# A two-layer decoder trunk in fp32: three of four MLP up blocks by seven quarter products per pair of units, and the MLP's weight sums on GpSimd

## The chip, the cores and the metric

One core of one Trainium2 chip. The metric is the device time of one execution, in microseconds (us). PE is TensorE, PEld its weight loads, DVE VectorE, ACT ScalarE, POOL GpSimd, SP SyncE, which here issues most DMAs.

## The reference

512 tokens, width 1024, two layers. Each layer ends in an MLP; the rest (a DeltaNet branch, a sliding-window attention branch, their merge) is not touched by the change.

```python
h2 = rmsnorm(x, pre_mlp_g)                                  # 512 x 1024
ff = jnp.square(jax.nn.relu(h2 @ w_ff1)) @ w_ff2            # 1024 -> 4096 -> 1024
return x + rmsnorm(ff, post_mlp_g)
```

## The kernel before

**Products.** All large products are fp32 work as three matmuls: an operand x is split into x_h (rounded by a cast) and x_l = x - x_h, and a product is wh·x_h + wh·x_l + wl·x_h. Weights come in chunks of 128 x 1024 (512 KB). Each goes the same way: a DMA by SP into a buffer `wr` (WR = 5 of them), a cast by ACT to `wh` (L323), a subtraction by DVE to `wl` (L324), then PE. `wh` and `wl` have LOOK = 4 buffers each, so a chunk's cast waits until PE has released the chunk four before it. `chunk_order` lists all chunks, `specs` is that list, and every `weights()` call takes the next prepared chunk and emits cast and subtraction of one further on.

**The MLP.** The 4096 middle columns are four stripes s = 0 to 3 of 1024. A stripe has an *up block*, the product with w_ff1: eight units of 128 middle columns, each 24 matmuls of 512 tokens (`mm_a`, L339 to L341), written to a PSUM bank of tag "pm" (two banks); ACT takes relu (L1374) and square (L1375) into a tile `raw`. In stripe 0 the first four units are made early, in two halves of 256 tokens (`mm_a2`, L350 to L352).

For s < 3 a *down stage* follows, the product with that stripe's 1024 rows of w_ff2. It is a Strassen-Winograd scheme over quarters of the activation and of the weights: seven products P1 to P7 instead of eight, each of two chunks, 168 matmuls in all (`mm_c`, L400 to L404). `lefts` makes the left operands from `raw` (S1 to S4 on DVE, each then split by an ACT cast L411 and a DVE subtraction L412). `seven` makes the right operands: sums of loaded chunks, eight DVE additions of 128 x 1024 per stage (L293). Results are accumulated into `acc` (L1332, L1389, L1393, L1401, L1403, L1409). Stripe 3 has a plain down product (`mm_b4` and `last_tiles`), whose operands `h3` are split in the up block.

**What sets the order.** Where no order is written out by hand (`Order`), the framework's scheduler orders each engine's instructions; an engine then runs its queue in that order and stops at an instruction whose inputs aren't there. A matmul into a PSUM bank waits until readers of that bank that are ahead of it in the program are done.

Of the kernel before, what the change touches and what calls it, by code (L numbers as in the profile page):

```python
# [41 lines left out]
WR = 5  # L42
FF_ORDER = (0, 4, 1, 5, 2, 6, 3, 7)
XB = 6

# [7 lines left out]
def chunk_order(depth):  # L53


    out = []
    for l in range(depth):
        a_in = lambda w, c: out.append(("chunk", w, l, 0, c, 0))
        b_in = lambda w, r, c, n: out.append(("chunk", w, l, r, c, n))
        for n in range(3):  # L60
            for j in range(4):
                b_in("w_in", j * 256, OFF_B + n * NB, NB)
        n_ = {"K": 0, "G": 0, "A": 0}
        for c in "".join(MIX):
# [12 lines left out]
        for m in range(KT):  # L77
            a_in("w_up_dn", m * P)
        for n in range(2):
            for j in range(4):  # L80
                b_in("w_o", j * 256, n * 512, 512)
        for s in range(4):
            for m in FF_ORDER if s < 3 else range(8):
                a_in("w_ff1", (s * 8 + m) * P)
            if s < 3:
                out.append(("seven", "w_ff2", l, s * 1024))
                continue
            for n in range(2):
                for j in range(4):
                    b_in("w_ff2", s * 1024 + j * 256, n * 512, 512)  # L90
    return out


def chunk_keys(depth):

    keys = {}
    for kind, *key in chunk_order(depth):
        if kind == "chunk":
            keys[tuple(key)] = None
        else:  # L100
# [19 lines left out]
def hybrid_trunk(ctx, tc, x, positions, pre_mix_g, dn_conv_w, dn_a_log, dn_dt_bias, dn_norm_g,  # L120
# [155 lines left out]

    def blocks(a, n_):
        return a[:, :2 * n_ if n_ else 1024].rearrange("p (k c) -> p k c", k=2 if n_ else 8)

    def seven(w, l, r0):  # L280
# [11 lines left out]
        def add(i, k, j):  # L292
            tt(out=held[j], in0=held[j], in1=part(i, k, j), op=ALU.add)  # L293
            return held[j]

        makes = (lambda j: take(0, 0, j),
                 lambda j: add(0, 1, j),
                 lambda j: add(1, 1, j),
                 lambda j: add(1, 0, j),
                 lambda j: (take(0, 1, j), add(1, 1, j))[1],  # L300
                 lambda j: part(1, 0, j),
                 lambda j: part(1, 1, j))
        return [(lambda f=f, j=j: f(j), 512) for f in makes for j in range(2)]


    specs = []
    for kind_, *key in chunk_order(depth):
        if kind_ == "seven":
            specs.extend(seven(*key))
        else:  # L310
            specs.append((tuple(key), key[4]))
# [3 lines left out]
    def prefetch(n, wr=None, sub=tt):  # L315
        while len(pre) < min(n, len(specs)):
# [5 lines left out]
            w = 2 * n_ if n_ else 1024  # L322
# [83 lines left out]

    def four(i):
        return [b("ps_b4") for b in ((PZ, PZ, PS, PS) if i % 2 else (PM, PM, PK, PS))]
# [34 lines left out]
    def norm_half(xt, gb, r, g):  # L443

        xs = T[7]("xs")
        stt(out=xs, in0=xt[:, g * 512:(g + 1) * 512], scalar=r, in1=gb[g], op0=ALU.mult, op1=ALU.mult)
        return xs
# [22 lines left out]
    def post_tiles(tiles, a0g, ps1, add1, q0, gb, xsrc, xdst, gb2=None):  # L470
# [4 lines left out]
        xt = [[T[5 + i]("xt") for i in range(2)] for t in tiles]  # L475
# [22 lines left out]
        if gb2 is not None:  # L498
            q = [(meansq(xo[i][:, :512], "nq0"), meansq(xo[i][:, 512:], "nq1")) for i in n]
            for i in n:  # L500
                r = rstd("nr", *q[i])
                xs.append([norm_half(xo[i], gb2, r, g) for g in range(2)])
# [17 lines left out]
    for l in range(depth):  # L520
# [817 lines left out]
        def ff2_tail(tiles, pss):  # L1338
            a0, a1 = [a[0] for a in acc], [a[1] for a in acc]
            if l == depth - 1:  # L1340
                post_tiles(tiles, a0, pss, a1, s0, gb3, xd, give)
            else:
                xs_next.extend(post_tiles(tiles, a0, pss, a1, s0, gb3, xd, keep, nxt[0]))

        def lefts(X, Y):

            a11, a21, a12, a22 = X[:, 0:512], X[:, 512:1024], Y[:, 0:512], Y[:, 512:1024]
            S = {n_: T[4](n_) for n_ in ("S1", "S2", "S3", "S4")}
            tt(out=S["S1"], in0=a21, in1=a22, op=ALU.subtract)
            tt(out=S["S2"], in0=a11, in1=S["S1"], op=ALU.subtract)  # L1350
            for name, U, src in (("P1", T[5], a11), ("P5", T[7], S["S1"]), ("P6", T[1], S["S2"]),
                                 ("P4", T[2], a22), ("P7", T[3], S["S3"]), ("P2", T[6], a12),
                                 ("P3", T[0], S["S4"])):
                if name == "P4":
                    tt(out=S["S4"], in0=a12, in1=S["S2"], op=ALU.subtract)
                    tt(out=S["S3"], in0=a21, in1=a11, op=ALU.subtract)
                p_ = pair(U, name)
# [3 lines left out]
        for s in range(3):  # L1361
            left = {f"P{i}": [] for i in range(1, 8)}
            raw = [None, None]
            for i, m in enumerate(FF_ORDER):
                if s == 0 and i < 4:
                    ps = early[i][0]
                else:
                    ps = PM("ps_f1")
                    mm_a(ps, h2)

                if i % 4 < 2:
                    raw[i % 2] = X4("raw")
                r_ = raw[i % 2].rearrange("p (a k n) -> p a k n", a=2, k=2)[:, :, m % 2, :]
                act(out=r_, in_=ps.rearrange("p (a n) -> p a n", a=2), func=AF.Relu)  # L1374
                act(out=r_, in_=r_, func=AF.Square)  # L1375
                if i % 4 == 3:
                    lefts(*raw)
            pa, pb_ = [PZ("ps_p1") for t in range(2)], [PS("ps_p5") for t in range(2)]
            mm_c(pa, left["P1"])
            v_ = [T[4]("p1") for t in range(2)]  # L1380
            for t in range(2):
                nc.scalar.copy(v_[t], pa[t])
            mm_c(pb_, left["P5"])
            for t in range(2):
                into(2 + t, 1, pb_[t])
            pc = [PS("ps_p6"), PK("ps_p6")]
# [7 lines left out]
            pc = [PM("ps_p4"), PM("ps_p4")]  # L1394
# [3 lines left out]
            pc = [PS("ps_p7"), PK("ps_p7")]  # L1398
# [5 lines left out]
            mm_c(pa, left["P2"], True)  # L1404
            for t in range(2):
                into(t, 0, pa[t])
            mm_c(pb_, left["P3"], True)
            for t in range(2):
                tt(out=acc[t][1], in0=pb_[t], in1=acc[t][1], op=ALU.add)  # L1409


        gb3 = gain(post_mlp_g[l])
        h3 = []
        for m in range(8):
            ps = PM("ps_f1")
            mm_a(ps, h2)
            r_ = T[4]("relu")
            act(out=r_, in_=ps, func=AF.Relu)
            act(out=r_, in_=r_, func=AF.Square)
            p_ = pair(T[m % 4], "h3")  # L1420
            split(r_, *p_)
            h3.append(p_)
# [43 lines left out]
```

## Time and profile before

| what | us |
|---|---|
| median of 3 runs (lowest to highest) | 1831.27 (1830.51 to 1831.94) |
| span of the profiled execution | 1828.6 |
| an up block of layer 0, stripes 1 to 3 | 43.5 each |
| a down stage of layer 0, stripes 1 and 2 | 38.6 each |
| PE busy in the span | 1809.1 |
| DVE, ACT, POOL busy | 1292.1, 940.9, 211.2 |

The profiled execution's own time is not listed apart from the three runs; its span lies 2.7 us under their median. A row of a timeline reads: start, length, engine, line, operation, output <- inputs, shape, and in brackets how long the engine had been idle and for what. A row of a group reads: busy us, mean ns of one, and the idle time ahead of them. PE's records overlap, since matmuls are pipelined: the step between starts is what one costs.

### The profile page before, as it was taken

To read this page: it belongs to the slowest core of one execution; us is meant where nothing else is said; L and a number is where in the kernel's file an instruction comes from. 1 tells how busy PE (TensorE), PEld (TensorE's weight loads), DVE (VectorE), ACT (ScalarE), POOL (GpSimd) and SP (SyncE) were. 2 spreads that over 40 slices of the span, in tenths; PEclk is the share of its full clock that TensorE was granted. 3 is DMA by queue.
4 is the path that set the end of the run, shared out by engine and by line. 5 is a ranking of instruction groups with operands and counts; after the bars stand their busy time and mean duration, and the time that the engine had idled before them with its cause. 6 is when DMAs were issued, how large, how long until landed. Compare 5 with 4: busy or idle time off the path is not lost.

```text
span 1828.6 us, 26748 instructions
## 1 busy us (share of the span) xinstructions
PE 1809.1 (99%) x9598; PEld 1503.9 (82%) x9598; DVE 1292.1 (71%) x2466; ACT 940.9 (51%) x1913; POOL 211.2 (12%) x386
## 2 busy tenths in 40 slices
PE   9999999999999999999999999999999999999998
PEld 8888778888788888888898887888887898888886
DVE  5499796887566758684556997968885568585934
ACT  6678742444434645544347877234444346554442
POOL 0322102221101000000003221022111010000000
PEclk9999999999999999999999999999999999999999
DMA  5633447554453363564245343485545534544631
GB/s 188 202 118 116 115 149 223 179 170 149 124 191 124 96 216 120 168 217 151 93 151 181 104 127 110 167 234 165 160 139 153 172 119 135 174 163 148 233 102 46
DMA packets 146422, 278.48 MB, mean 152 GB/s; under 512 B 33569, under 2 KB 66657, under 8 KB 146290
## 3 DMA queue, kind: packets, MB, share of 16 engines
q1 hardware_dynamic: 145778, 276.75, 47.4%
q8 instruction: 75, 1.23, 0.3%
q14 instruction: 57, 0.47, 0.1%
q0 software_dynamic: 512, 0.03, 0.0%
HBM read 239.38 MB, written 37.36 MB: 151 GB/s over the span
## 4 chain that ended last, share of the span: by engine, by line
PE 84%; DVE 6%; ACT 5%; DMA 3%; issue 1%; POOL 1%; SPq 0%; POOLq 0%; DVEq 0%; ACTq 0%
PE ps_f L340 6%; PE ps_f L339 6%; PE ps_f L341 6%; PE ps_p L402 3%; PE ps_p L404 3%; PE ps_p L400 3%; PE ps_b L388 3%; PE ps_b L387 3%; PE ps_b L389 3%; PE ps_vp L339 2%; PE ps_us L339 2%; PE ps_ud L339 2%; PE ps_vp L341 2%; PE ps_ud L341 2%; PE ps_ud L340 2%; PE ps_us L340 2%
## 5 line engine op out<-in xcount | busy, mean ns | idle before, releaser
L323 ACT CAST wh<-wr 128x1024 fp32r<-128x1024 f32 (+1 forms) x332 | 343.1, 1040 | 542.2 <-PE ps_f L340 145.8
L324 DVE TENSOR_TENSOR wl<-wr,wh 128x1024 fp32r<-128x1024 f32 (+1 forms) x332 | 400.4, 1216 | 303.6 <-ACT wh L323 300.6
L339 PE MATMUL ps_f<-g_h,wh 128*128 128x512 f32 x448 | 174.3, 389 | 0.0
L340 PE MATMUL ps_f<-g_l,wh 128*128 128x512 f32 x448 | 174.3, 389 | 0.0
L341 PE MATMUL ps_f<-g_h,wl 128*128 128x512 f32 x448 | 174.3, 389 | 0.0
L402 PE MATMUL ps_p<-wl,P_h 128*128 128x512 f32 x336 | 131.4, 391 | 0.4 <-DVE wl L324 0.3
L404 PE MATMUL ps_p<-wh,P_l 128*128 128x512 f32 x336 | 130.8, 389 | 0.0
L400 PE MATMUL ps_p<-wh,P_h 128*128 128x512 f32 x336 | 129.5, 389 | 0.0
L437 POOL TENSOR_TENSOR pr<-pq,pw 128x1 f32<-128x1 f32 x16 | 9.8, 613 | 807.6 <-DVE pq L436 807.6
L339 PEld LDWEIGHTS ps_f<-g_h,wh 128*128 128x128 f32 x448 | 84.1, 188 | 17.4
L341 PEld LDWEIGHTS ps_f<-g_h,wl 128*128 128x128 f32 x448 | 84.1, 188 | 17.4
L340 PEld LDWEIGHTS ps_f<-g_l,wh 128*128 128x128 f32 x448 | 84.1, 188 | 17.4
L402 PEld LDWEIGHTS ps_p<-wl,P_h 128*128 128x128 f32 x336 | 63.1, 188 | 15.8 <-DVE wl L324 2.4
L400 PEld LDWEIGHTS ps_p<-wh,P_h 128*128 128x128 f32 x336 | 63.1, 188 | 13.3
L404 PEld LDWEIGHTS ps_p<-wh,P_l 128*128 128x128 f32 x336 | 63.1, 188 | 12.8
L387 PE MATMUL ps_b<-wh,h_h 128*128 128x432 f32 (+1 forms) x192 | 71.1, 370 | 0.0
L388 PE MATMUL ps_b<-wl,h_h 128*128 128x432 f32 (+1 forms) x192 | 70.5, 367 | 0.3 <-DVE wl L324 0.3
L389 PE MATMUL ps_b<-wh,h_l 128*128 128x432 f32 (+1 forms) x192 | 70.2, 366 | 0.0
L293 DVE TENSOR_TENSOR wr<-wr 128x1024 f32<-128x1024 f32 x48 | 58.0, 1220 | 2.6 <-DMA wr<-in_weights_dram 1.9
L340 PE MATMUL ps_qp<-h_l,wh 128*128 128x512 f32 x128 | 54.0, 422 | 0.0
L339 PE MATMUL ps_vp<-h_h,wh 128*128 128x512 f32 x128 | 53.9, 421 | 0.0
L341 PE MATMUL ps_vp<-h_h,wl 128*128 128x512 f32 x128 | 53.6, 419 | 0.0
(359 smaller groups left out, 4873.6 us busy)
## 6 DMA issues: line engine op xcount, KB each, us to landing
wr<-in_weights_dram SPq DMA_DIRECT2D x320, 512.0 KB, 3.5
wr<-in_weights_dram SPq DMA_DIRECT2D x24, 432.0 KB, 3.6
D<-dd SPq DMA_DIRECT2D x32, 256.0 KB, 3.2
xd<-xo SPq DMA_DIRECT2D x12, 512.0 KB, 2.8
xt<-xd SPq DMA_DIRECT2D x24, 256.0 KB, 3.7
D<-gd SPq DMA_DIRECT2D x16, 256.0 KB, 6.5
dd<-D SPq DMA_DIRECT2D x16, 256.0 KB, 3.9
kkd<-kk SPq DMA_DIRECT2D x16, 256.0 KB, 2.0
```

The lines of the kernel that those rows point to most:

```text
L293: tt(out=held[j], in0=held[j], in1=part(i, k, j), op=ALU.add)
L323: nc.scalar.copy(wh[:, :w], wr[:, :w])
L324: sub(out=wl[:, :w], in0=wr[:, :w], in1=wh[:, :w].bitcast(F32), op=ALU.subtract)
L339: mm(ps, lhsT=wh[:, k, :], rhs=hi, start=k == 0, stop=False)
L340: mm(ps, lhsT=wh[:, k, :], rhs=lo, start=False, stop=False)
L341: mm(ps, lhsT=wl[:, k, :], rhs=hi, start=False, stop=k == KT - 1)
L387: mm(pss[t], lhsT=hi[:, tsl], rhs=wh[:, r, :], start=k == 0, stop=False)
L388: mm(pss[t], lhsT=hi[:, tsl], rhs=wl[:, r, :], start=False, stop=False)
L389: mm(pss[t], lhsT=lo[:, tsl], rhs=wh[:, r, :], start=False, stop=k == KT - 1)
L400: mm(pss[t], lhsT=hi[:, c], rhs=wh[:, r, :], start=first, stop=False, skip_group_check=onto)
L402: mm(pss[t], lhsT=hi[:, c], rhs=wl[:, r, :], start=False, stop=False, skip_group_check=onto)
L404: mm(pss[t], lhsT=lo[:, c], rhs=wh[:, r, :], start=False, stop=last, skip_group_check=onto)
```

## The change

Stripes 1 to 3 get `ff1_pairs` in place of eight `mm_a`. Two units (256 middle columns) and two halves of 256 tokens make a 2 x 2 scheme of quarters: the weights' quarters are halves of the 1024 inputs by unit, the tokens' operands are a11, a12, a22 (quarters of h2, split already) and four combinations n1 to n4. Each of the seven products (`mm_h`) has 12 matmuls of 256, so a pair has 84 of them, and a block 336 of 256 instead of 192 of 512.

The results that several quarters share are not added by DVE but continued in PSUM: ACT copies A's result a0 into one of two "seed" banks (y, L1461), D is added onto it there, ACT copies that into the other seed bank (z, L1470), and so on. Two more matmuls of 512 per layer start the seed banks. q0 (product F) stands in the second half of the bank that holds a0 (except in a block's first pair, where it has a bank of its own) and is copied to SBUF (L1467, L1476). The products B and C of a pair are made after A of the next one (`finish`).

Weights: of each pair two raw chunks are loaded, and GpSimd makes four sums of 128 x 512 from them (L336, `paired`); four chunks go to PE per pair: one raw, two of sums, and a half one ("tail"). The sums in `seven` go from DVE to GpSimd too (L304). WR is 7 instead of 5.

The combinations: `combos` makes them in stripe 0 by eight GpSimd additions of 128 x 1024 per layer, with splits on ACT and DVE; n4 takes the place of h2's fourth quarter.

In the down stage P2 moves from sixth to third place; of P2, P7 and P3 the splits for both halves are now emitted inside the down stage (`make_later`); other PSUM tags and other tile tags (T[...]) are used.

```diff
-WR = 5
+WR = 7
+PAIRS = (((0, 1), (4, 5), (2, 3), (6, 7)), ((0, 1), (2, 3), (4, 5), (6, 7)))
...
         def add(i, k, j):
-            tt(out=held[j], in0=held[j], in1=part(i, k, j), op=ALU.add)
+            ptt(out=held[j], in0=held[j], in1=part(i, k, j), op=ALU.add)
...
+    def paired(l, s):
...
+                    for o_, i0, i1 in ((ya, x0, x2), (yb, ya, x3), (yd, x2, x3), (yc, yb, x1)):
+                        ptt(out=o_, in0=i0, in1=i1, op=ALU.add)
...
+        for n, ms in enumerate(PAIRS[s == 3]):
+            raw, fa, fb, tail = one(*ms)
+            out.append((raw, 0))
+            if last:
+                out.append((last, -1))
+            out += [(fb, 0), (fa, 0)] if n == 0 else [(fa, 0), (fb, 0)]
+            last = tail
...
+    def mm_h(ps, w, k0, op, start):
+
+        wh, wl = w
+        for k in range(4):
+            hi, lo = op[k]
+            mm(ps, lhsT=wh[:, k0 + k, :], rhs=hi, start=start and k == 0, stop=False,
+               skip_group_check=True)
+            mm(ps, lhsT=wh[:, k0 + k, :], rhs=lo, start=False, stop=False, skip_group_check=True)
+            mm(ps, lhsT=wl[:, k0 + k, :], rhs=hi, start=False, stop=k == 3, skip_group_check=True)
...
+        def ff1_pairs(done):
...
+            for n, ms in enumerate(PAIRS[s == 3]):
+                R = X4("raw")
+                y, z = (b[:, half(n % 2)] for b in seeds)
+                ps = PM("ps_f1")
+                a0, q0 = ps[:, half(0)], ps[:, half(1)]
+                q_ = sm.tile([P, 256], F32, name="q7")
+                c1 = weights()
+                mm_h(a0, c1, 0, ops["a11"], True)
+                nc.scalar.copy(y, a0)
+                finish()
+                if n == 0:
+                    q0 = PM("ps_f1")[:, half(1)]
+                    c3 = weights()
+                    mm_h(q0, c3, 4, ops["n3"], True)
+                    nc.scalar.copy(q_, q0)
+                c2 = weights()
+                mm_h(y, c2, 4, ops["n2"], False)
+                nc.scalar.copy(z, y)
+                mm_h(a0, c1, 4, ops["a12"], False)
+                act(out=R[:, half(0)], in_=a0, func=AF.Relu)
+                if n > 0:
+                    c3 = weights()
+                    mm_h(q0, c3, 4, ops["n3"], True)
+                    nc.scalar.copy(q_, q0)
+                mm_h(z, c2, 0, ops["n1"], False)
+                stt(out=R[:, half(3)], in0=z, scalar=-1.0, in1=q_, op0=ALU.mult, op1=ALU.subtract)
+
+                def finish(n=n, ms=ms, R=R, y=y, z=z, q_=q_, c3=c3):
+                    mm_h(y, c3, 0, ops["a22"], False)
+                    tt(out=R[:, half(2)], in0=y, in1=q_, op=ALU.add)
+                    act(out=R[:, 512:], in_=R[:, 512:], func=AF.Relu)
+                    mm_h(z, weights(), 0, ops["n4"], False)
+                    act(out=R[:, half(1)], in_=z, func=AF.Relu, scale=-1.0)
+                    act(out=R, in_=R, func=AF.Square)
+                    done(n, ms, R)
+            finish()
```

What stands on the engines, at three places. First ACT's queue in the up block of stripe 1, layer 0. Before (line 323 is a weight cast, 1374 and 1375 relu and square of a unit, 411 the cast of a down operand):

```order
L323 CAST wh_7220<-wr_7218 128x1024
L1374 ACTIVATE raw_7147<-ps_f1_7184 128x2x256
L1375 ACTIVATE raw_7147<-raw_7147 128x2x256
L411 CAST P1_h_7256<-raw_7147 128x512
L323 CAST wh_7289<-wr_7287 128x1024
L1374 ACTIVATE raw_7181<-ps_f1_7217 128x2x256
L1375 ACTIVATE raw_7181<-raw_7181 128x2x256
```

In the changed kernel, from the second pair's copy of D into z to the third pair's copy of F (373 is a weight cast, 471 the cast of a down operand; ps_f1_7371 is the bank that holds the third pair's a0 and q0):

```order
L373 CAST wh_7373<-wr_7335 128x1024
L1483 ACTIVATE raw_7248<-raw_7248 128x512
L373 CAST wh_7408<-wr_7404 128x1024
L1485 ACTIVATE raw_7248<-seed_7154 128x256
L1486 ACTIVATE raw_7248<-raw_7248 128x1024
L1470 COPY seed_7154<-seed_7153 128x256
L471 CAST P4_h_7442<-raw_7248 128x512
L373 CAST wh_7448<-wr_7284 128x512
L471 CAST P5_h_7433<-S1_7430 128x512
L471 CAST P6_h_7438<-S2_7431 128x512
L1472 ACTIVATE raw_7370<-ps_f1_7371 128x256
L1476 COPY q7_7372<-ps_f1_7371 128x256
```

A unit's relu stood directly behind one cast. Now the relu of a0 (L1472) stands behind ten instructions that belong to the pair before and to later chunks.

Second, PE's queue at the place of that relu, in the fourth pair of the same block. First before, at the border of two units:

```order
L340 MATMUL ps_f1_7184<-g_l_5939,wh_7098 128x512
L341 MATMUL ps_f1_7184<-g_h_5938,wl_7099 128x512
L339 MATMUL ps_f1_7217<-g_h_5936,wh_7119 128x512
L340 MATMUL ps_f1_7217<-g_l_5937,wh_7119 128x512
L341 MATMUL ps_f1_7217<-g_h_5936,wl_7120 128x512
```

And in the changed kernel, at the border of E (operands g, bank ps_f1_7515) and F (operand n3, the same bank); two matmuls of the next down stage (line 450) stand between them:

```order
L464 MATMUL ps_f1_7515<-g_l_5939,wh_7408 128x256
L465 MATMUL ps_f1_7515<-g_h_5938,wl_7409 128x256
L450 MATMUL ps_p1_7687<-wh_7568,P1_h_7426 128x512
L450 MATMUL ps_p1_7688<-wh_7568,P1_h_7426 128x512
L462 MATMUL ps_f1_7515<-n3_h_6637,wh_7517 128x256
L464 MATMUL ps_f1_7515<-n3_l_6638,wh_7517 128x256
L465 MATMUL ps_f1_7515<-n3_h_6637,wl_7518 128x256
```

Two units followed each other in different banks. F follows E in the bank that L1472 reads in between.

Third, the weight sums in the down stage of stripe 1, layer 0. Before, on DVE (324 is a chunk's subtraction, 293 a sum of two chunks, 412 a down operand's low part):

```order
L412 TENSOR_TENSOR P7_l_7275<-S3_7252,P7_h_7274 128x512
L293 TENSOR_TENSOR wr_7321<-wr_7321,wr_7388 128x1024
L324 TENSOR_TENSOR wl_7358<-wr_7355,wh_7357 128x1024
L293 TENSOR_TENSOR wr_7355<-wr_7355,wr_7461 128x1024
L324 TENSOR_TENSOR wl_7392<-wr_7321,wh_7391 128x1024
L293 TENSOR_TENSOR wr_7321<-wr_7321,wr_7480 128x1024
```

In the changed kernel, on POOL:

```order
L304 TENSOR_TENSOR wr_7566<-wr_7566,wr_7644 128x1024
L304 TENSOR_TENSOR wr_7598<-wr_7598,wr_7691 128x1024
L304 TENSOR_TENSOR wr_7566<-wr_7566,wr_7757 128x1024
L304 TENSOR_TENSOR wr_7598<-wr_7598,wr_7786 128x1024
L304 TENSOR_TENSOR wr_7847<-wr_7847,wr_7849 128x1024
L304 TENSOR_TENSOR wr_7566<-wr_7566,wr_7805 128x1024
L304 TENSOR_TENSOR wr_7598<-wr_7598,wr_7828 128x1024
L304 TENSOR_TENSOR wr_7882<-wr_7882,wr_7884 128x1024
L336 TENSOR_TENSOR wr_7969<-wr_7943,wr_7945 128x512
L336 TENSOR_TENSOR wr_7970<-wr_7945 128x512
```

The same eight sums of a stage stand in a row on POOL, and the next block's pair sums (L336) behind them; DVE keeps the subtractions.

More of the change, by code (lines that the diff above doesn't have):

```diff
@@ L1409, in hybrid_trunk, with done @@
                 tt(out=acc[t][1], in0=pb_[t], in1=acc[t][1], op=ALU.add)
+            if s == 0:
+                next(cg, None)
+        s = 3
         gb3 = gain(post_mlp_g[l])
[L1413 to L1422, printed above, removed]
+        h3 = [None] * 8
+        def done(n, ms, R):
+            for i, m in enumerate(ms):
+                h3[m] = pair(T[(1, 2, 5, 7)[m % 4]], "h3")
+                split(R.rearrange("p (a k n) -> p a k n", a=2, k=2)[:, :, i, :],
+                      *(a.rearrange("p (a n) -> p a n", a=2) for a in h3[m]))
+        ff1_pairs(done)
         pss = four(1)
```

193 lines of the change are left out of this document (145 added, 48 removed).

## The prediction

> **What bounds the kernel now.** I read the page first, then the busy time of each engine stage by stage (the table of windows), then PE's waits. The page's heads and the first row of its chain:
>
> ```profile
> span 1828.6 us, 26748 instructions
> ...
> PE 1809.1 (99%) x9598; PEld 1503.9 (82%) x9598; DVE 1292.1 (71%) x2466; ACT 940.9 (51%) x1913; POOL 211.2 (12%) x386
> ...
> PEclk9999999999999999999999999999999999999999
> ...
> PE 84%; DVE 6%; ACT 5%; DMA 3%; issue 1%; POOL 1%; SPq 0%; POOLq 0%; DVEq 0%; ACTq 0%
> ```
>
> TensorE never stands still and never loses its clock. The table of windows, for layer 0: the up block of stripe 1, its down stage, and the up block of stripe 3.
>
> ```profile
> core 0: us, PE busy (x) PEld busy (x) DVE busy (x) ACT busy (x) POOL busy (x), PEclk, DMA share, GB/s
> 664.17:707.69 43.52, 43.52 (x194) 36.04 (x192) 21.66 (x25) 20.80 (x31) 0.00 (x0) 1.00 0.34 106
> 707.69:746.25 38.56, 38.37 (x169) 31.40 (x168) 37.28 (x45) 19.63 (x24) 0.00 (x0) 1.00 0.58 196
> ...
> 828.33:871.85 43.52, 43.52 (x194) 36.04 (x192) 15.95 (x18) 20.70 (x30) 0.00 (x0) 1.00 0.39 135
> ```
>
> An up block is bound by PE alone: 43.52 us for 192 matmuls of 512, 226.7 ns each, DVE and ACT half idle. In the down stage DVE is busy 97% (37.28 of 38.56 us): no room there. From 575 to 900 us, which holds the MLP of layer 0, PE's waits are all of these:
>
> ```profile
> PE ps_p L402 <- DVE wl L324: 0.3, 2, 0.2
> PE ps_n L457 <- DVE g_l L463: 0.2, 1, 0.2
> ```
>
> So whatever shortens PE's stream in an up block shortens the kernel, as long as nobody makes PE wait; and any wait added there is paid in full.
>
> **The saving.** Six up blocks go from 192 matmuls of 512 to 336 of 256. What a 256 wide one costs stands in the early units' stream on PE (the ends are modelled, so I read starts):
>
> ```profile
> 578.82 0.28 PE L350 MATMUL ps_f<-g_h,wh 128*128 128x256 f32 x1
> ...
> 585.89 0.28 PE L352 MATMUL ps_f<-g_h,wl 128*128 128x256 f32 x1
> ...
> 589.53 0.36 PE L350 MATMUL ps_f<-g_h,wh 128*128 128x256 f32 x1
> 589.73 0.28 PE L351 MATMUL ps_f<-g_l,wh 128*128 128x256 f32 x1
> ```
>
> From the first to the second row are 59 steps in 7.07 us: 119.8 ns, a little over half of 226.7. So 336 x 0.1198 = 40.25 us against 43.52: 3.27 us less in a block, 19.6 in six. A product (12 matmuls) lasts 1.44 us. The last two rows show the first step after a stop, 0.20 instead of 0.12 us.
>
> The Trainium skill ("TensorE: Matmul & The Clock Gate", Back-to-back issue gap) lists 262 cycles for a 256 wide matmul and 518 for 512. At its 2.4 GHz that would be an estimated 109.2 and 215.8 ns and a saving of 28 us. The trace disagrees with both figures (119.8 and 226.7), and the sum goes by the trace.
>
> The two seed matmuls per layer add 4 x 0.227 = 0.9 us.
>
> **The waits that come, in the up blocks.** The order lists seven products per pair of units. I call them by their right operand: A (a11), B (a22) and C (n4) of the pair before, D (n2), E (a12), F (n3), G (n1). In the later three pairs of a block two of them wait for ACT.
>
> B adds into the seed bank into which ACT has just copied A's result (L1461). F writes the second half of the PSUM bank whose first half ACT must first read, with the relu of E's result (L1472). In ACT's queue this relu stands behind everything that B, C, D and E release. ACT's steps have these rows: a timeline of stripe 1 of before, and two groups.
>
> ```profile
> 691.33 0.62 ACT L411 CAST P_h<-S 128x512 fp32r<-128x512 f32 x1 [0.58 <-DVE S L1355]
> 691.85 0.59 ACT L1374 ACTIVATE raw<-ps_f 128x512 f32<-128x512 f32 x1
> 692.34 1.05 ACT L323 CAST wh<-wr 128x1024 fp32r<-128x1024 f32 x1
> 693.28 0.62 ACT L411 CAST P_h<-S 128x512 fp32r<-128x512 f32 x1
> 693.80 0.63 ACT L1375 ACTIVATE raw<-raw 128x512 f32<-128x512 f32 x1
> ...
> 697.73 0.59 ACT L1374 ACTIVATE raw<-ps_f 128x512 f32<-128x512 f32 x1
> 698.36 0.64 ACT L1375 ACTIVATE raw<-raw 128x512 f32<-128x512 f32 x1
> ```
>
> ```profile
> L899 ACT COPY M<-ps_s 128x256 f32<-128x256 f32 x48 | 16.6, 374 | 7.2 <-PE ps_s L893 6.6
> ```
>
> An independent successor starts 0.10 us before the record ends (cast of 1024: 0.94 from start to start, cast of 512: 0.52), a dependent one 0.04 after it. What passes between engines, from two timelines:
>
> ```profile
> 577.22 0.40 PE L361 MATMUL ps_wo<-wh,mT_l 128*128 128x512 f32 x1
> 577.46 0.39 PE L359 MATMUL ps_wo<-wh,mT_h 128*128 128x512 f32 x1
> 577.72 0.60 ACT L431 ACTIVATE jk<-ps_wo 128x512 bf16<-128x512 f32 x1 [0.29 <-PE ps_wo L361]
> ```
>
> ```profile
> 433.26 0.35 DVE L1176 SCALAR_TENSOR_TENSOR rr<-ps_ks,neg,vs 128x128 f32<-128x128 f32 x1
> ...
> 433.75 0.41 PE L1179 MATMUL ps_y<-rr,Pt 128*128 128x128 f32 x2
> ```
>
> From the end of PE's stream (577.46) to ACT 0.26 us; from the end of a result (433.61) to PE 0.14.
>
> Now one pair, from the end of B. ACT casts the next weight chunk into the slot that B frees (0.95), relu of half the pair before (0.53), the cast that waits for C (0.95), relu of a quarter (0.37 and 0.03, since the next reads it: 0.40), the square of 1024 (no row; as the cast, 0.95), the copy z of D's result (0.27), a P1 or P4 cast (0.52), the 512 wide tail cast that waits for E (0.52), and the relu, 0.37 to its end. That is 5.46; with 0.26 ahead and 0.14 behind, 5.86 us. PE in that time has C, D and E, 4.31 us. F waits 1.55. B waits 0.26 + 0.37 + 0.14 = 0.77 behind A. Two restarts add 0.16. Together 2.48 us a pair, and the pair lasts 12.54 us instead of 10.06. In the third pair of stripes 1 and 2 the casts P5 and P6 stand in that queue too (2 x 0.52): 3.52. In stripe 3 one more cast of 512: 3.00 in each pair. The first pair has its q0 in another bank and other work between A and D: nothing.
>
> A block of stripe 1 or 2: 40.25 + 2.48 + 3.52 + 2.48 = 48.73, which is 5.21 over 43.52; stripe 3: 49.25, 5.73 over. A layer 16.15, both layers **+32.3 us**: the 19.6 are in that sum and are eaten. ACT as a whole has room; it is one chain in series that doesn't. Bounds: at worst the full recorded lengths, without the overlap of 0.10 (8 of them a pair, +0.8 x 18 pairs = +14); at best F's wait hidden by a shorter queue (-1.55 x 18 = -28).
>
> **The shared work of DVE and GpSimd.** In the down stages the sums of 1024 (L293) go from DVE to GpSimd, with four sums of 512 for the next block's first pair. DVE's groups in the down stage of the table above:
>
> ```profile
> L324 DVE TENSOR_TENSOR wl<-wr,wh 128x1024 fp32r<-128x1024 f32 x14 | 16.5, 1216 | 2.4 <-ACT wh L323 2.4
> L293 DVE TENSOR_TENSOR wr<-wr 128x1024 f32<-128x1024 f32 x5 | 6.0, 1218 | 0.2 <-DMA wr<-in_weights_dram 0.2
> L1332 DVE TENSOR_TENSOR acc<-ps_p,acc 128x512 f32<-128x512 f32 x6 | 4.0, 680 | 0.0
> L412 DVE TENSOR_TENSOR P_l<-S,P_h 128x512 fp32r<-128x512 f32 x4 | 2.7, 684 | 0.0
> ...
> L1389 DVE TENSOR_TENSOR p<-ps_p,p 128x512 f32<-128x512 f32 x2 | 1.4, 682 | 0.0
> ...
> L1401 DVE TENSOR_TENSOR p<-ps_p,p 128x512 f32<-128x512 f32 x2 | 1.3, 679 | 0.0
> ```
>
> GpSimd's groups of additions or products over the whole run, and two places where such a one met a DVE subtraction:
>
> ```profile
> L1108 POOL TENSOR_TENSOR qe<-qq,egb 128x512 f32<-128x512 f32 x16 | 20.5, 1282 | 34.3 <-DVE qq L718 26.3 <-PE ps_i L1015 7.1
> ...
> L828 POOL TENSOR_TENSOR rt<-qt,cs 128x128 f32<-128x128 f32 x8 | 3.7, 462 | 0.0
> ```
>
> ```profile
> 466.30 1.27 POOL L1108 TENSOR_TENSOR qe<-qq,egb 128x512 f32<-128x512 f32 x1 [3.91 <-PE ps_i L1015]
> ```
>
> ```profile
> 466.53 2.13 DVE L324 TENSOR_TENSOR wl<-wr,wh 128x1024 fp32r<-128x1024 f32 x1
> ```
>
> ```profile
> 77.57 1.27 DVE L324 TENSOR_TENSOR wl<-wr,wh 128x1024 fp32r<-128x1024 f32 x1 [3.21 <-ACT wh L323]
> ```
>
> ```profile
> 77.63 1.30 POOL L830 TENSOR_TENSOR kv<-rt 128x16 f32<-128x16 f32 x1
> 78.89 0.22 POOL L831 TENSOR_TENSOR kv<-rt 128x16 f32<-128x16 f32 x1
> ```
>
> In the first place the subtraction took 2.13 instead of 1.22: it ran only once GpSimd was done. In the second, the other way round, a GpSimd operation of 16 columns took 1.30, the next 0.22. So an operation of DVE with both inputs in SBUF and one of GpSimd exclude each other. By the slope of the two GpSimd groups, (1.282 - 0.462) / 384 columns, one of 1024 takes an estimated 2.37 us, twice what DVE needs.
>
> DVE in such a stage: 37.28 less 6.0, and three lows more (P2, P7, P3 are split later): 33.3. Of it 6.7 read PSUM (L1332, L1389, L1401) and need not wait; 26.6 remain. GpSimd: seven sums of 1024 and four of 512, 21.7. Together 48.3 us, one after the other, in a stage of 38.56: 9.8 too much. Against it: casts run three chunks (3 x 2.75 us) ahead of PE, less cast and subtraction 2.27, leaves 6.0 of slack; and the sums of 512 (5.1) are needed only afterwards. Between 0 and 9.8 us, then; below nothing is out, since PE idles only 0.2 there now. I take 3, nearest to 9.8 - 6.0, for stripes 1 and 2 (four stages) and 0.5 for stripe 0 (two), where ACT takes part of the accumulation: 13. The backlog then makes the next block's first pair late, 0 to 3 us; 1 each, 6. Together **+19 us**, from 0 to 65.
>
> Edits at nothing: the eight GpSimd combinations (19 us a layer) lie beside 21.66 us of DVE in an up block of 43.52, and fit; if they delay a subtraction over the slack, 2 us a layer. Seven load buffers instead of five, the other tile tags, the scratch size and P2's earlier place cost PE no instruction.
>
> **The sum.** The profiled execution spans 1828.6 us, 2.7 under the median of the runs, which I take as what lies around it: 1831.3 + 32.3 + 0.9 + 19 = **1883.5 us**.
>
> **The rivals.**
>
> *Waits hidden (faster).* If the relu of E's result and the copy of A's were done when F and B come up, PE would keep its stream: 1831.3 - 19.6 + 0.9 = 1812.6. It decides at 4.31 us, what C, D and E cover of ACT's 5.86. For it: ACT is 48% busy in up blocks. Against: the order's queue. 0.08.
>
> *ACT's chain alone.* GpSimd's sums fit in the slack: 1831.3 + 32.3 + 0.9 = 1864.5. For it: POOL is idle in these stages now and all its inputs are loaded early. 0.14.
>
> *Shared work is the bound.* Each down stage of stripes 1 and 2 takes 9.8 more, of stripe 0 5, each first pair 3: 1864.5 + 39.2 + 10 + 18 = 1932. 0.13.
>
> *The clock falls.* PE's waits, 1.55 to 2.6 us, might cost granted clock, which stood at 1.00 without such waits. 3.4 us at half speed behind each of 18 pairs' waits cost 1.7 each, 31 us: 1914. The Trainium skill ("TensorE: Matmul & The Clock Gate", Part 1: The HAM clock gate) has the clock halved after an idle window of about 3.4 us; by that rule waits as short as these leave it full, and no run here shows it. 0.03.
>
> *It doesn't do what it says.* The order shows all 336 matmuls and 16 sums per block, so 0.02 for about 1831.
>
> **How the numbers follow.** My own case has 0.60 and runs from 1850 (port free, queue shorter) to 1905. The range reaches into the bound by shared work, 1850 to 1925, and leaves out the faster rival, no effect and that rival's end. About 0.2% (3.7 us) is what a measurement of this kernel can tell from no change. Faster 0.08, same 0.02, slower 0.90.
>
> **What would show it.** In the profile after: PE's waits list F's line (L462) for ACT's relu L1472, near 1.5 us, 18 times, and for the copy L1461, 0.8 us; up blocks near 49 us; steps of 0.12 us in between; L374 on DVE well over 1.22 us on average, and PE waiting for it in the down stages at 41 us. It is wrong if PE's share stays at 99%, if up blocks are under 43.5, or if the down stages lose more than the up blocks.

## The result and the profile after

| | median us | runs | ratio, 95% interval |
|---|---|---|---|
| before | 1831.53 | 1830.51 to 1831.94 | |
| changed | 1965.45 | 1962.97 to 1967.51 | 1.0729 [1.0714, 1.0744] |

The change is slower, as forecast, but by 134 us and not by 52: outside the range of 1850 to 1925. The page of the changed kernel, its heads and two of its groups:

```profile
span 1963.0 us, 29090 instructions
...
PE 1843.1 (94%) x10466; PEld 1562.8 (80%) x10466; DVE 1448.0 (74%) x2528; ACT 1004.2 (51%) x2047; POOL 554.4 (28%) x546
...
PEclk9999999999999999999999999999999999999899
...
L374 DVE TENSOR_TENSOR wl<-wr,wh 128x1024 fp32r<-128x1024 f32 (+2 forms) x380 | 518.5, 1374 | 202.7 <-ACT wh L373 198.5
...
...
L304 POOL TENSOR_TENSOR wr<-wr 128x1024 f32<-128x1024 f32 x48 | 135.1, 2830 | 177.1 <-DVE wl L374 132.3
```

PE's share fell from 99 to 94%, and what it is busy with takes longer although 19.6 us of matmul time are gone. The mean subtraction of 1024 columns (L374) rose from 1.23 to 1.44 us; the row's 1.37 holds narrower ones too. The clock's row of 40 slices shows almost nothing of what matters: a slice is 49 us. The table of windows does, here for layer 0: the rest of stripe 0's up block, its down stage, the up block and the down stage of stripe 1.

```profile
core 0: us, PE busy (x) PEld busy (x) DVE busy (x) ACT busy (x) POOL busy (x), PEclk, DMA share, GB/s
...
604.32:631.78 27.46, 23.69 (x99) 19.14 (x98) 24.04 (x21) 14.86 (x23) 16.67 (x7) 0.94 0.27 87
631.78:674.58 42.80, 40.72 (x172) 32.97 (x170) 37.05 (x33) 25.38 (x36) 27.30 (x12) 0.96 0.44 136
674.58:729.77 55.19, 45.53 (x339) 44.02 (x338) 34.18 (x39) 27.89 (x47) 19.55 (x13) 0.94 0.36 113
729.77:776.48 46.71, 41.99 (x169) 33.20 (x168) 46.64 (x39) 21.76 (x28) 30.49 (x13) 0.93 0.44 138
```

Before, the four took 21.8, 38.4, 43.5 and 38.6 us at a clock of 1.00. Every stage lost, also stripe 0's up block, whose matmuls the change doesn't touch. PE's waits over the whole run:

```profile
PE ps_f L465 <- DVE wl L374: 24.6, 6, 4.6
PE ps_f L462 <- ACT raw L1472: 20.8, 12, 2.2
PE ps_p L454 <- DVE P_l L472: 10.4, 4, 2.6
PE ps_p L452 <- DVE wl L374: 9.3, 9, 3.1
PE seed L462 <- ACT seed L1461: 9.0, 18, 0.5
PE ps_f L389 <- ACT raw L1532: 7.5, 2, 3.8
```

The second and the fifth row are the chain that the prediction had worked out (L1472 and L1461). The first, third and fourth are its "shared work", and larger. The sixth is a wait in stripe 0's up block that it had put at nothing.

To size everything in one measure I went through the starts of PE's matmuls in the MLP and took each step's excess over its undisturbed length (0.227 us for 512, 0.120 for 256), as a wait if it is over twice that length, else as slow running:

| where the 134 us come from | forecast | measured |
|---|---|---|
| shorter stream, and seeds | -19.6 and 0.9 | -19.6 and 0.9 |
| waits for ACT's chain (copy, relu; in a block's fourth pair the next stage's matmuls ahead of F) | 51.9 with restarts | 42.5 |
| waits at a block's first pair | 6 | 26.3 |
| waits in down stages | 13 | 32.1 |
| wait in stripe 0's up block | 0 | 8.2 |
| slow steps: clock, and some 5 of restarts | 0 | 42.2 |
| sum | 52.2 | 132.6 |

How the third pair's F in stripe 1 waits, in the timelines of ACT (whose queue holds the P5 and P6 casts there, the row with x2) and of PE:

```profile
703.26 1.05 ACT L373 CAST wh<-wr 128x1024 fp32r<-128x1024 f32 x1 [1.72 <-PE seed L464]
704.22 0.62 ACT L1483 ACTIVATE raw<-raw 128x512 f32<-128x512 f32 x1
704.74 1.03 ACT L373 CAST wh<-wr 128x1024 fp32r<-128x1024 f32 x1
705.69 0.37 ACT L1485 ACTIVATE raw<-seed 128x256 f32<-128x256 f32 x1
706.09 1.06 ACT L1486 ACTIVATE raw<-raw 128x1024 f32<-128x1024 f32 x1
707.06 0.37 ACT L1470 COPY seed<-seed 128x256 f32<-128x256 f32 x1
707.36 0.61 ACT L471 CAST P_h<-raw 128x512 fp32r<-128x512 f32 x1
707.88 0.61 ACT L373 CAST wh<-wr 128x512 fp32r<-128x512 f32 x1
708.39 1.13 ACT L471 CAST P_h<-S 128x512 fp32r<-128x512 f32 x2
709.43 0.37 ACT L1472 ACTIVATE raw<-ps_f 128x256 f32<-128x256 f32 x1
```

```profile
707.33 0.28 PE L465 MATMUL ps_f<-g_h,wl 128*128 128x256 f32 x1
709.86 0.38 PE L462 MATMUL ps_f<-n_h,wh 128*128 128x256 f32 x1 [2.25 <-ACT raw L1472]
```

ACT runs without a gap from 703.26 to 709.80, in the very order of the queue; E's stream ends at 707.45, so L1472 could start some 0.26 us later; it starts at 709.43. PE waits 2.41 us over the usual step (forecast 2.59).

How a left operand of the down stage waits for GpSimd, from the timelines of POOL, DVE and ACT at the start of stripe 1's:

```profile
732.92 6.22 POOL L304 TENSOR_TENSOR wr<-wr 128x1024 f32<-128x1024 f32 x2 [1.16 <-DVE wl L374]
```

```profile
734.02 2.90 DVE L1506 TENSOR_TENSOR S<-raw 128x512 f32<-128x512 f32 x1
736.95 2.74 DVE L1508 TENSOR_TENSOR S<-raw,S 128x512 f32<-128x512 f32 x1
739.62 0.68 DVE L472 TENSOR_TENSOR P_l<-raw,P_h 128x512 fp32r<-128x512 f32 x1
```

```profile
736.95 0.62 ACT L471 CAST P_h<-S 128x512 fp32r<-128x512 f32 x1 [1.69 <-DVE S L1506]
739.73 0.62 ACT L471 CAST P_h<-S 128x512 fp32r<-128x512 f32 x1 [2.15 <-DVE S L1508]
```

Two operations of 0.68 us took 2.90 and 2.74, each until the GpSimd sum beside it was done; after the second sum (739.14) DVE's operations take 0.68 again. S2 needs S1, and P5's low part stands behind both on DVE, so PE waited 2.76 us for it.

The casts and subtractions of the same stage (729.77 to 776.48), as groups:

```profile
L374 DVE TENSOR_TENSOR wl<-wr,wh 128x1024 fp32r<-128x1024 f32 x13 | 26.4, 2042 | 0.0
...
L373 ACT CAST wh<-wr 128x1024 fp32r<-128x1024 f32 x14 | 14.6, 1049 | 20.4 <-POOL wr L304 10.8 <-PE ps_p L454 5.4 <-POOL wr L336 4.2
```

A subtraction took 2.04 us instead of 1.22, and ACT stood 15.0 us until GpSimd had a sum ready.

In stripe 0's up block GpSimd makes the combinations. ACT's queue there, with the relu (L1532) for which PE waited 3.9 us:

```profile
612.48 0.63 ACT L1426 ACTIVATE n_h<-hs 128x512 fp32r<-128x512 f32 x1 [2.45 <-POOL hs L1436]
...
615.84 0.62 ACT L471 CAST P_h<-S 128x512 fp32r<-128x512 f32 x1 [1.69 <-DVE S L1506]
...
618.52 0.59 ACT L1532 ACTIVATE raw<-ps_f 128x512 f32<-128x512 f32 x1
```

And the clock, in PE's starts at the first pair of stripe 1:

```profile
676.13 0.28 PE L464 MATMUL ps_f<-n_l,wh 128*128 128x256 f32 x1
680.08 0.39 PE L465 MATMUL ps_f<-n_h,wl 128*128 128x256 f32 x1 [3.68 <-DVE wl L374]
...
680.55 0.31 PE L465 MATMUL ps_f<-n_h,wl 128*128 128x256 f32 x1
...
681.30 0.41 PE L462 MATMUL ps_f<-n_h,wh 128*128 128x256 f32 x1
681.51 0.41 PE L464 MATMUL ps_f<-n_l,wh 128*128 128x256 f32 x1
```

The wait is 3.8 us over a step. 0.6 us after it the steps go from 0.12 to 0.21 and stay there until 684.1; the granted clock is 0.50 from 680.65 to 684.06.

### The profile page after: what moved, and what is told of

It is laid out like the page before. It is cut to its first block, busy times and chain, and to the rows that moved or that the text cites. A ratio compares the mean times of both kernels' runs of the same rounds, so it can differ in the third digit from the quotient of the medians.

```text
span 1963.0 us, 29090 instructions
## 1 busy us (share of the span) xinstructions
PE 1843.1 (94%) x10466; PEld 1562.8 (80%) x10466; DVE 1448.0 (74%) x2528; ACT 1004.2 (51%) x2047; POOL 554.4 (28%) x546
## 5 line engine op out<-in xcount | busy, mean ns | idle before, releaser
L374 DVE TENSOR_TENSOR wl<-wr,wh 128x1024 fp32r<-128x1024 f32 (+2 forms) x380 | 518.5, 1374 | 202.7 <-ACT wh L373 198.5
L373 ACT CAST wh<-wr 128x1024 fp32r<-128x1024 f32 (+2 forms) x380 | 383.6, 1013 | 491.4 <-POOL wr L304 62.4
L336 POOL TENSOR_TENSOR wr<-wr 128x512 f32<-128x512 f32 x96 | 162.5, 1713 | 116.1 <-DMA wr<-in_weights_dram 90.6
L304 POOL TENSOR_TENSOR wr<-wr 128x1024 f32<-128x1024 f32 x48 | 135.1, 2830 | 177.1 <-DVE wl L374 132.3
L462 PE MATMUL seed<-g_h,wh 128*128 128x256 f32 x192 | 56.2, 293 | 9.0 <-ACT seed L1461 9.0
L462 PE MATMUL seed<-n_h,wh 128*128 128x256 f32 x192 | 59.7, 311 | 0.0
L464 PE MATMUL seed<-n_l,wh 128*128 128x256 f32 x192 | 59.2, 308 | 0.0
L465 PE MATMUL seed<-n_h,wl 128*128 128x256 f32 x192 | 58.9, 307 | 0.0
L465 PE MATMUL ps_f<-n_h,wl 128*128 128x256 f32 x96 | 32.1, 335 | 24.6 <-DVE wl L374 24.6
L462 PE MATMUL ps_f<-g_h,wh 128*128 128x256 f32 x192 | 54.7, 285 | 0.0
```

What stands on the lines that cost most here:

```text
L304: ptt(out=held[j], in0=held[j], in1=part(i, k, j), op=ALU.add)
L336: ptt(out=o_, in0=i0, in1=i1, op=ALU.add)
L373: nc.scalar.copy(wh[:, :w], wr[:, :w])
L374: sub(out=wl[:, :w], in0=wr[:, :w], in1=wh[:, :w].bitcast(F32), op=ALU.subtract)
L462: mm(ps, lhsT=wh[:, k0 + k, :], rhs=hi, start=start and k == 0, stop=False, skip_group_check=True)
L465: mm(ps, lhsT=wl[:, k0 + k, :], rhs=hi, start=False, stop=k == 3, skip_group_check=True)
```

## The experiments

The theory: three costs, ACT's chain, DVE and GpSimd excluding each other, and a clock that falls behind the longer of the waits that these two make. The rivals are named at each.

**Without weight sums.**

```diff
         def add(i, k, j):
-            ptt(out=held[j], in0=held[j], in1=part(i, k, j), op=ALU.add)
-            return held[j]
+            return part(i, k, j)
...
+                    b["a"], b["b"] = b["0"], b["1"]
...
-                        ptt(out=o_, in0=i0, in1=i1, op=ALU.add)
```

> The changed kernel without any weight sum: neither the pair sums nor the sums of the down stage are made, the loaded chunks are used as they are (this part of the computation is left out; everything else runs). Theory: the loss of 131 us is 42 of ACT's chain, 66 of waits that come from GpSimd and DVE excluding each other, 42 of a clock that falls behind waits of more than some 2 us, less the 19.6 of the shorter stream. Without sums the down stages return to 38.5 us and the first pair of a block waits for nothing; ACT's waits, 7 us a block, and the 4 us in stripe 0's up block stay, with part of the clock: 1877 us, 1865 to 1890. Rival, the clock falls because of the 256 wide stream itself and not of waits: granted clock in the up blocks stays at 0.94 and the time is near 1900. Rival, ACT's chain and not the sums is what makes the down stages late: they stay over 42 us, and the time over 1920.

Measured: 1870.4 us, 1.0214 [1.0199, 1.0230]. The up block and the down stage of stripe 1, and PE's largest waits:

```profile
670.34:718.57 48.23, 42.31 (x340) 41.00 (x338) 26.12 (x35) 27.98 (x47) 0.00 (x0) 1.00 0.31 99
718.57:756.22 37.65, 37.65 (x168) 31.17 (x167) 34.61 (x44) 21.82 (x28) 0.00 (x0) 1.00 0.64 210
```

```profile
PE ps_f L458 <- ACT raw L1468: 20.4, 12, 2.2
PE seed L458 <- ACT seed L1457: 9.0, 18, 0.5
```

The down stage waits for nothing, the first pair neither, and ACT's waits stand at the size that they had. The block takes 48.2 us; the prediction had worked out 48.7 for exactly this, a block with ACT's chain alone. The 256 wide stream runs at 1.00, so it isn't the stream that lowers the clock. The 2.4 us waits are still there and didn't lower it in this run.

The traces show what parts the two kernels. Through a run the granted clock is 1.00 or 0.50, and it changes only at points that lie 3.413 us, or a multiple of that, apart: all 23 falls in the MLPs of the changed kernel lie on one such grid. Cut at these points, here is the 2.4 us wait for the third pair's F in stripe 1, first in the changed kernel (707.45 to 709.86), then in this one (697.76 to 700.14):

```profile
707.96:711.37 3.41, 1.51 (x12) 1.51 (x13) 3.41 (x6) 1.85 (x5) 0.00 (x0) 1.00 0.66 202
711.37:714.78 3.41, 3.41 (x18) 3.41 (x17) 1.27 (x3) 1.12 (x2) 0.00 (x0) 0.50 0.37 105
```

```profile
695.62:699.03 3.41, 2.30 (x20) 2.10 (x18) 2.97 (x5) 3.38 (x7) 0.00 (x0) 1.00 0.01 2
699.03:702.45 3.42, 2.31 (x19) 2.31 (x20) 3.42 (x6) 1.43 (x4) 0.00 (x0) 1.00 0.00 0
702.45:705.86 3.41, 2.91 (x24) 2.71 (x24) 1.69 (x3) 1.41 (x2) 0.00 (x0) 1.00 0.50 155
```

In the first kernel 1.90 us of the wait lay in one stretch, and the next stretch ran at half the clock. In the second the wait was cut into 1.27 and 1.11 us, and nothing followed. By PE's starts the same holds all through the MLPs of these two kernels: every stretch at the full clock with more than 1.90 us of idle PE was followed by one at 0.50, and none with less than 1.88 was. In the other runs' traces three stretches, with 1.94 to 2.05 us idle, are exceptions.

**F in a bank of its own.**

```diff
                 if n > 0:
+                    q0 = PZ("ps_f1")[:, half(1)]
                     c3 = weights()
```

> The changed kernel with F's result in a bank of its own in every pair, not only in a block's first. Theory: F no longer waits for the relu of E's result, 1.4, 2.4 and 1.2 us a block go (31 us in all), the copy's waits before B (0.66 each) stay, and the clock that falls behind the 2.4 us wait comes back, some 10 us: 1924 us, 1915 to 1940. Rival, ACT as a whole is late and the wait moves to G or to the next pair's B: no change, 1955 to 1970.

Measured: 1923.3 us, 1.0502 [1.0480, 1.0524]: 42 us less, 1 beside the forecast. The waits for L1472 are gone from PE's list and none took their place in the up blocks. In PE's starts of a block only the first pair's wait (2.9 to 4.5) and three of 0.66 are left. But the four down stages of stripes 1 and 2 now take 47.9 to 50.4 us instead of 46.7 to 50.2, 5.7 us more in sum: some of what is saved is lost behind.

**All sums on DVE.**

```diff
-            ptt(out=held[j], in0=held[j], in1=part(i, k, j), op=ALU.add)
+            tt(out=held[j], in0=held[j], in1=part(i, k, j), op=ALU.add)
...
-                        ptt(out=o_, in0=i0, in1=i1, op=ALU.add)
+                        tt(out=o_, in0=i0, in1=i1, op=ALU.add)
```

> The changed kernel with all weight sums on DVE instead of GpSimd (the combinations of stripe 0 stay on GpSimd). Theory: nothing excludes DVE in the down stages, a sum of 1024 takes 1.22 us instead of 2.8, and DVE has room in the up blocks: down stages 38.5 to 40 us, the first pair's wait under 1 us, as without sums: 1880 us, 1868 to 1900. Rival, the sums are too much for DVE, which was 97% busy in the down stages before: stages of 42 us and more, 1900 to 1930. Rival, it is not the exclusion that costs but that sums stand ahead of a block's first pair at all: no more than 10 us better than the changed kernel.

Measured: 1905.7 us, 1.0405 [1.0390, 1.0421]. Better by 60 us, not by 85: my theory gave 1880, and the time is the first rival's, though the stages took 41 us and not 42 and more. Stripe 1's down stage:

```profile
719.95:760.92 40.97, 39.02 (x169) 30.86 (x167) 40.70 (x51) 19.60 (x26) 0.00 (x0) 1.00 0.50 154
```

DVE is busy for 40.70 of 40.97 us. It took 37.28 before; eight sums are back, the four of the next first pair and three lows are new. Nothing excludes DVE any more, it is full. The first pairs of stripes 2 and 3 still wait 3 us.

**Combinations later.**

```diff
-                    if i in (1, 2, 3):
+                    if i in (3, 5, 7):
```

> The changed kernel with the combinations of stripe 0 begun after the fourth, sixth and eighth unit instead of the second, third and fourth. Theory: ACT's queue stands at a cast that waits for GpSimd's combinations, and relu of the units behind it, so PE waits 4 us once per layer and then runs slowly for 3.4 us; later combinations are spread and that goes: 8 us of waits and 3 of clock, 1954 us, 1948 to 1960. Rival, the combinations then collide with the down stage's sums and come back there as a later first pair: 1960 to 1975.

Measured: 1970.2 us, 1.0758 [1.0740, 1.0776], 5 more than the changed kernel. Stripe 0's up block returned to 21.8 us, and its down stage went from 42.8 to 51.3: the rival, to the letter except that it came back in the down stage already.

**One part alone, in the kernel before: the down stages' sums on GpSimd.**

```diff
-            tt(out=held[j], in0=held[j], in1=part(i, k, j), op=ALU.add)
+            ptt(out=held[j], in0=held[j], in1=part(i, k, j), op=ALU.add)
```

> The kernel before with one part of the change alone: the down stages' weight sums (L293) on GpSimd instead of DVE. No seven-product up blocks, no ACT chain, no pair sums. Theory: DVE and GpSimd exclude each other, so a stage holds some 24.6 us of DVE with two SBUF inputs and 16.6 to 19 of GpSimd, 41 to 44 us in 38.5, with 6 us of slack: the down stages of stripes 1 and 2 take 41 to 45 us, with one fall of the clock each, and the kernel is slower by 8 to 35 us, 1850 as the likeliest. Rival, GpSimd only unburdens DVE (28% of it is free, and POOL was idle): 1826 to 1833. The up blocks stay at 43.5 us and 1.00 in either case.

Measured: 1860.4 us, 1.0160 [1.0145, 1.0175], 29 us slower, in the theory's span and far from the rival. A down stage and the sums' group:

```profile
712.21:755.44 43.23, 39.59 (x169) 31.14 (x168) 37.10 (x40) 20.01 (x24) 15.10 (x5) 1.00 0.54 177
```

```profile
L293 POOL TENSOR_TENSOR wr<-wr 128x1024 f32<-128x1024 f32 x48 | 134.9, 2816 | 341.7 <-DVE wl L324 286.0 <-issue 26.5 <-DMA wr<-in_weights_dram 15.9
```

DVE lost the sums and is still busy 37.10 us (37.28 before): its own operations took some 5.6 us longer than before in that stage, beside GpSimd's sums. The up block ahead of it stayed at 43.52. ACT also stood 13.1 us there for GpSimd's sums, and a sum takes 2.8 us on GpSimd and 1.22 on DVE. How much of the 29 us is the exclusion and how much only the longer sum ahead of a cast, this run doesn't part.

**Three things undone: own bank, sums on DVE, later combinations.** The diffs above, together.

> The changed kernel with three things undone together: F's result in a bank of its own, the sums on DVE, the combinations of stripe 0 later. Theory, that the costs add up: 1905.7 with the sums on DVE alone, less some 31 of F's waits and 5 of clock, less 5 to 11 in stripe 0: 1862 us, 1850 to 1875. The first pair's wait and down stages of 41 us stay, since DVE is full there. Rival, F's waits give DVE the time that the sums need, so that the down stages and the first pairs get worse by what is saved: over 1880.

Measured: 1868.0 us, 1.0198 [1.0181, 1.0215]. The costs add up as the theory has it. Stripe 1's up block takes 42.6 us, for the first time less than before.

**PE's order changed as well.** E goes ahead of D, C ahead of B (in `finish`).

```diff
+                mm_h(a0, c1, 4, ops["a12"], False)
+                act(out=R[:, half(0)], in_=a0, func=AF.Relu)
                 mm_h(y, c2, 4, ops["n2"], False)
                 nc.scalar.copy(z, y)
-                mm_h(a0, c1, 4, ops["a12"], False)
-                act(out=R[:, half(0)], in_=a0, func=AF.Relu)
```

> As the kernel with three things undone, and PE's order in a pair changed to A, C and B of the pair before (C first), E, D, F, G: C covers the copy before B, E covers the low part of the pair before ahead of D. Theory: the 18 waits of 0.66 us go, 12 us: 1850 us, 1838 to 1862; up blocks of stripe 1 near 41 us, that is under the 43.5 of before. Rival, DVE is the bound by now: no change against the kernel without this order, 1858 to 1870.

Measured: 1877.4 us, 1.0254 [1.0238, 1.0269]: 9 slower than without, against both expectations. The second pair takes 10.07 us from start to start, as it should. But C now stands directly behind A and waits for DVE's reading of z in the last pair, 1.9 us. With other such steps PE waits 3.2 us in stripe 1's block, against 2.0 without the new order, and in layer 0 the blocks of stripes 2 and 3 each have one more stretch at half the clock. The rest of the 9 us stays open. I had counted what the new order covers and not what it uncovers.

**With the combinations on DVE, early.** In `combos`, `ptt` becomes `tt`.

> As the kernel with the changed order, but with the combinations of stripe 0 at their early place and on DVE: no GpSimd work in the MLP at all. Theory: a combination takes 1.22 us instead of 2.8 and 3.4, the casts behind it wait less, and stripe 0's up block is at 21.8 to 23 us with no fall of the clock: 4 to 8 us better than with late ones on GpSimd. Rival, the chain of combinations through ACT's queue holds up the relu in any case: up block 25 us or more, no better.

Measured: 1871.1 us, 1.0217 [1.0202, 1.0232], 6 better, as the theory said: stripe 0's up block takes 23.5 us, a little over the 23 expected, and its down stage 38.1.

**Sums of 512 on GpSimd, sums of 1024 on DVE.** Only `add` in `seven` is undone.

> The changed kernel with the down stages' sums of 1024 back on DVE, the pair sums of 512 left on GpSimd: parts the two groups of sums. Theory: the eight sums of 1024 are the larger part of the exclusion; the down stages fall from 46 to 40 to 42 us, the first pair's wait stays at 3 us or more, since its four sums still meet DVE at its busiest: 1908 us, 1895 to 1925. Rival, the pair sums alone hold DVE up as much: over 1935. Rival, without the four sums on DVE it beats the version with all sums there: under 1895.

Measured: 1925.4 us, 1.0516 [1.0502, 1.0530], just beyond the upper end of 1925. The down stages fell to 40.7 to 41.1 us as expected; the first pairs of stripes 2 and 3 got worse, 5.5 us of wait. Their four sums now meet a DVE that is full, which is the likely reason and was not tested by itself.

**A version meant to win: first pair plain.** The first pair by two `mm_a`, the other three as with the own bank, all sums and combinations on DVE, n4 in tiles of its own, five load buffers.

```diff
+                if n == 0:
+                    for k, m in enumerate(ms):
+                        ps = PM("ps_f1")
+                        mm_a(ps, h2)
...
+                    done(n, ms, R)
+                    continue
```

> A version meant to beat both: the first pair of each block as two plain units of 24 matmuls of 512 (no sums for it, so DVE has no sums of 512 in the down stages and nothing of a block's start waits for them), the other three by seven products with F in a bank of its own, all sums and combinations on DVE, five load buffers as before, n4 in tiles of its own. A block: 10.88 + 3 x 10.06 + 2 copies' waits of 0.66 and little more, 42.6 us against 43.5; down stages 38.5 to 39 (DVE at 97% again); stripe 0 1.4 us longer. Theory: 1829 us, 1823 to 1838, about what the kernel before takes. Rival, DVE's queue in its order holds weights up in the down stages even without the sums of 512: stages of 40 us and more, with falls of the clock, 1845 to 1865.

Measured: 1845.1 us, 1.0077 [1.0064, 1.0089]. The best of the versions that compute everything, and still slower than before. The up block and the down stage of stripe 2:

```profile
750.93:794.46 43.53, 42.10 (x302) 39.45 (x300) 32.29 (x45) 25.56 (x42) 0.00 (x0) 1.00 0.36 114
794.46:835.19 40.73, 39.10 (x171) 31.29 (x170) 40.73 (x50) 21.85 (x28) 0.00 (x0) 1.00 0.63 202
```

No gain in the up block, and DVE full in the down stage: the rival, and for a reason that I should have seen in part. Against the table of before DVE has the three lows more that the change moved there (2.1 us), and seven of the eight sums fall into the stage instead of five (2.4 us).

**Only PE and ACT, in the changed order, and in the change's own order.** Both without sums (left out), with the own bank and the combinations on DVE.

> The changed kernel without weight sums (left out, in pairs and down stages), F in a bank of its own, the changed order of C, B, E, D, and the combinations on DVE: what is left of the change is the shorter stream on PE and ACT's work. Theory: the three costs are all that there is; a block takes 40.3 to 41.5 us, stripe 0 1.4 us more than before, the clock stays at 1.00: 1831.5 - 19.6 + 0.9 + 2.8, with some 3 for single waits: 1818 us, 1813 to 1826. Rival, ACT's work has no room in a pair of 10.06 us even in a good order: blocks over 43 us, 1830 and more.

> The changed kernel without weight sums (left out, in pairs and down stages), F in a bank of its own, the combinations on DVE, and PE's order in a pair as the change has it. Theory: each block keeps three copies' waits of 0.66 and restarts, 42.6 us against 43.5 before, the down stages stand at 38.3, stripe 0 is 1.6 us longer: two layers 2 x (1.6 - 3 x 0.9) and 0.9 of seeds, 1830 us, 1826 to 1833, so that the change could not gain 0.2% even if its sums were free. Rival, the order of the kernel without sums before it was the only thing that ate the saving: 1815 to 1822.

Measured: 1834.3 us, 1.0018 [1.0009, 1.0027], and 1827.3 us, 0.9980 [0.9971, 0.9989]. The first came out at the rival's numbers, over 1830 and with blocks of 44 to 46 us, but not for its reason, ACT's time: of PE's waits 7.0 us, in four, are for DVE's reading of z and 4.9, in ten, for ACT's copy, and the second kernel does the same work of ACT in blocks of 42.6. The second came out as expected. Its largest wait in the MLP is

```profile
PE seed L458 <- ACT seed L1457: 9.0, 18, 0.5
```

the copy before B. So with every sum for free and F's wait gone, the change would be worth 4 us.

## Why the prediction was wrong

The sum missed by 80 us: 42 for slow steps, most of it the clock, 39 for the shared work and 8 in stripe 0 were missing, and ACT's chain was 9 too dear.

- **The direction and ACT's chain: right, and shown.** F's wait by L1472's place in the queue (forecast 1.55 and 2.59, measured 1.38 and 2.41), B's (0.77, measured 0.66), the saving by steps of 0.120, a block of 48.7 (measured 48.2 without sums). The own bank took away 42 us.
- **Shared work: the mechanism right, the term mis-sized.** The prediction took 19 us from a span of 0 to 65. The waits at first pairs and in down stages came to 58. The step that failed here is "leaves 6.0 of slack". I subtracted the lead of the weight casts from the surplus of 9.8 us. But a cast whose input is a GpSimd sum has no such lead: in stripe 1's down stage ACT stood 15.0 us for sums. And the left operands S1, S2 and their splits have none at all; they are made just when PE needs them, and each waited for a whole GpSimd sum. The down stages' sums alone, put on GpSimd in the kernel before, cost 29 us.
- **"Edits at nothing" failed for the combinations.** I added up busy time (19 + 21.66 us in 43.52). The whole work fits; but the window that matters is the 22 us behind the early units, and in it ACT's casts of the combinations, and of S1 and S2, which waited for GpSimd or for a DVE held up by it, stand in the queue ahead of a unit's relu. That made 8.2 us of waits, and more through the clock.
- **The clock: a rival at 0.03 that happened.** Slow steps cost 42.2 us, some 5 of them restarts after a wait; the clock stood at 0.50 for 85 us. The step that failed is the term left out of the sum: "The clock falls" stood beside it as a case of 0.03, since waits of 1.55 to 2.6 us were taken to be too short. What counted was the idle time within one stretch of 3.41 us, and 1.9 us of it was enough (the rows shown with the run without sums). All 13 waits of more than 2.75 us in the changed kernel, most of them of the shared work, were followed by a fall. A wait of 2.4 us was or wasn't, by its place on the grid: of the four in the changed kernel three were, of the four without sums none. That ACT's waits alone left the clock at 0.997 there was in part luck. The Trainium skill ("TensorE: Matmul & The Clock Gate", Part 1: The HAM clock gate) names an idle window of about 3.4 us, free-running; the trace agrees with the length, 3.413 us, and with places that no wait shifts, but the window need not be idle throughout: 1.9 us were enough here.
- **The cases were kept apart that belong together.** "Shared work is the bound" gave 1932, "the clock falls" 31 us more. One causes the other: together 1963, against 1965 measured. That the two meet so closely is luck: in that sum the shared work and ACT's chain are each 9 us too dear, the clock is 11 short and stripe 0's 8 are missing. With a chance of its own for each and none for both, the range ended at 1925.

## What to carry to other kernels

Where PE is the bound at 99%, a scheme with fewer matmuls is worth only what its dependences leave: here 19.6 us of matmuls against handoffs through PSUM copies that take 12 us even with all else for free. Before work goes to an idle engine, ask whether it shares something with the busy one: twice the time on GpSimd, exclusive with DVE, made DVE's own operations longer, and a busy share doesn't tell that from work. And when a forecast holds waits of some microseconds, add what TensorE's clock makes of them, as a consequence and not as another case; here that hung on how much idle time came together within 3.4 us.

## What the hardware showed that I had not expected

- DVE with two SBUF inputs and GpSimd took turns, operation by operation, in the timelines read here: DVE operations of 0.68 us took 2.74 to 2.90, and GpSimd's sums of 1024 took 2.83 on average, against 2.41 where one stood alone.
- PE's steps slow not at the end of a wait but at the next point of a grid of 3.413 us: 0.6 us after the wait of 3.8 us, 1.5 us after the one of 2.4. A fall lasts one such stretch, here twice two. It costs an estimated 1.5 us, from 16 steps of 0.213 us where 28 of 0.120 would fit.
- Moving the same GpSimd work to another place moved the wait and its size with it (21.8 and 51.3 us instead of 27.5 and 42.8).
